# One layer of a hybrid encoder on one core: the Hyena branch's last gate and output kept with channels on partitions, its RMS factor applied when the output projection leaves PSUM

## The chip, the core and the metric

The kernel runs on one core of a Trainium2 chip. The core has a matrix engine (TensorE, PE in the profile; its weight loads are a row of their own, PEld), a vector engine (VectorE, DVE), a scalar engine (ScalarE, ACT), GpSimd (POOL), which here only issues DMAs that add into their destination or load weights, and SyncE (SP), which issues most of the other DMAs. All five run their own list of instructions in order and wait for each other by semaphores. Matmuls write into PSUM; everything else lives in SBUF, on 128 partitions, or in DRAM.

The metric is the device time of one execution in microseconds (us), as the median of several.

## The reference, cut to what matters

Sequence length 1024, model width 1024, batch 1, all in float32. Both branches are 512 channels wide; each is RMS-normalised over its 512 channels, multiplied by a SiLU gate, and the two together go through one output projection that is added to the input.

```python
h = rms_norm(x, norm_g[l]); proj = h @ w_in[l]
...
u = centred_short_conv(hy_in, conv_w[l], conv_b[l])      # 3 taps
hv, hx1, hx2 = jnp.split(u, 3, axis=-1)
...
z = hx1 * long_conv(hv, k_f[:, 0], hb[0])                # FFT convolution
z = hx2 * long_conv(z, k_f[:, 1], hb[1])
y_h = z
...
y = jnp.concatenate([rms_norm(y_h, hy_out_norm_g[l]) * jax.nn.silu(g_h),
                     rms_norm(y_a, attn_out_norm_g[l]) * jax.nn.silu(g_a)], axis=-1)
x = x + y @ w_out[l]
```

`rms_norm(y_h, g)` is `y_h * rsqrt(mean(y_h**2) + eps) * g`. The factor 1 / rms is one number per token; `g` and the gate act per channel. Since the output projection sums over channels, a factor per token may be applied to the projected row as well.

## The kernel before

**Stages.** `prelude` loads x and makes its high and low float32r parts (a float32 product is made of three float32r matmuls: high times high, high times low, low times high; L257 to L259 for the channel tiles, L508 to L510 for queries, keys and values, L1124 to L1126 for the output projection). Then the input projection runs over 12 Hyena tiles of 128 channels (3 parts n of 4 channel quarters s), 3 query/key/value tiles and 8 gate tiles. At the same time the "branch" runs: for each of four channel quarters the spectrum of the implicit filter, two long convolutions as matmuls with DFT tables (`fw` L761 forward, `inv` L802 inverse, butterflies and products on VectorE), and after the fourth quarter the attention. At the end comes the output projection (`output_part`), 8 token blocks by 2 halves of 512 columns by 2 branches.

**Order.** The program is written as two Python generators, the branch and the projections, that `weave` (L1177) merges: each yields a planned cost, and the branch goes on while `ta * SHARE <= tb + LEAD`. A list scheduler with priorities then places the instructions of each engine in a fixed order. `EARLY` attention units are emitted before the four `hyena_output` calls, and each call yields `HC`. The last three gate tiles are computed together; behind them on POOL's queue stand the loads of the output weights (`woraw`, L1031 and L1049). The attention goes on beside the output projection: each attention unit asks `self.outs` for one more output part. Below, an attention block means the work from one query block's `bT` transposes (L960) to the next one's.

**Tiles of the change.** `short_conv` (L406) makes a Hyena tile with channels on the 128 partitions in `hsc`. Its closure `transposes` (L429), kept in `put_off` and run by `late` one tile later, turns it to tokens on partitions: 8 PE transposes into PSUM (`uT`, L434), two ACT copies (L439) and a store to DRAM (`hy`, L440), from which the branch loads it as `u` (L817). `long_conv` (L750) multiplies the inverse transform by the gate (L803) with tokens on partitions; `hyena_quarter` (L807) squares the result on ACT in 8 instructions with a sum over channels (`zsq`, `zssq`, L834) and stores it (`zd`). `hyena_output` (L1066) loads gate and `zd`, applies SiLU (L1064), multiplies by 1 / rms (L1075), turns the result back by 8 PE transposes (`yT`, L1079), multiplies by channel weight and gate out of PSUM (L1081) and splits into high and low parts `yh` (L1084) and `yl` (L1085). 1 / rms is made at L1288 from `zssq`. `output_part` (L1112) gives the first `FIRST` = 3 token blocks a bank of their own for the Hyena half, which leaves PSUM by itself; for the other five blocks both branches are added up in one bank and leave it once (L1128).

## Time and profile before

| what | value |
|---|---|
| median of 3 runs | 638.59 us (636.98 to 641.66) |
| the profiled execution's own time | 637.56 us |
| its span, from the first to the last instruction | 635.8 us |
| granted TensorE clock | 1.0 all through |
| PE transposes: `uT` / `yT` / `oT` | 96 / 32 / 32 |
| DMA | 98.37 MB, mean 155 GB/s |

A row of a group of instructions reads: line of the kernel, engine, operation, output <- inputs, shapes, count, then busy time in us and the mean duration of one in ns, then the idle time of the engine ahead of them and who ended it. A matmul's duration is longer than the distance to the next one's start, since matmuls overlap in the engine; the chain of waits shows the distances.

### The profile page before, as it was taken

Reading aid. Unit: us, or ns where it says so; the run is one execution under the profiler, and the core shown is the slowest. Engines: PE = TensorE matmul, PEld = TensorE weight load, DVE = VectorE, ACT = ScalarE, POOL = GpSimd, SP = SyncE. Lnnn points to the kernel's source line nnn. Section 1 sums busy time; section 2 is a strip of 40 time slices with the busy share of each in tenths; the row PEclk is TensorE's granted clock in tenths of the full one; section 3 lists DMA queues with packets and bytes.
Section 4 is the critical chain, followed back from the end, with each engine's and each line's share of the span. In section 5 each row is a group of like instructions: output and inputs, shape, how many; then the busy total and the mean of one; then the engine's idle time right before and its main releaser. Section 6 shows DMA issues by size and latency. Waiting matters only on the chain.

```text
span 635.8 us, 10699 instructions
## 1 busy us (share of the span) xinstructions
PE 625.0 (98%) x3994; PEld 553.1 (87%) x3994; DVE 531.2 (84%) x1189; ACT 266.5 (42%) x506; POOL 65.3 (10%) x83
## 2 busy tenths in 40 slices
PE   9999999999999999999999999999998999999997
PEld 7878998989898989899998988888787878888885
DVE  6969699997999997979999899689989888976531
ACT  6766413254432353523443332545465343544210
POOL 0121002021100121211102102100200000000000
PEclk9999999999999999999999999999999999999999
DMA  8966937478574576694548656645645125313321
GB/s 324 281 148 155 296 86 181 126 180 202 147 182 129 148 184 160 138 216 107 134 135 208 184 175 156 188 138 182 207 137 179 56 65 166 105 37 114 100 82 51
DMA packets 47107, 98.37 MB, mean 155 GB/s; under 512 B 6728, under 2 KB 15440, under 8 KB 46800
## 3 DMA queue, kind: packets, MB, share of 16 engines
q1 hardware_dynamic: 32784, 63.79, 30.2%
q0 software_dynamic: 10720, 26.21, 21.8%
q10 hardware_dynamic: 3552, 7.71, 3.5%
q8 instruction: 31, 0.51, 0.3%
q14 instruction: 20, 0.16, 0.1%
HBM read 53.65 MB, written 22.02 MB: 119 GB/s over the span
## 4 chain that ended last, share of the span: by engine, by line
PE 85%; DMA 5%; DVE 4%; issue 3%; ACT 2%; POOL 0%; SPq 0%; POOLq 0%; ACTq 0%; DVEq 0%
PE proj L257 10%; PE proj L258 9%; PE proj L259 9%; PE dft L645 8%; PE pv L1000 5%; PE fw L761 5%; PE po L1124 4%; PE po L1126 4%; PE po L1125 4%; PE inv L802 4%; PE qkv L508 3%; PE qkv L509 3%; PE qkv L510 3%; PE smax L940 1%; PE uT L434 1%
## 5 line engine op out<-in xcount | busy, mean ns | idle before, releaser
L257 PE MATMUL proj<-h,w_hi 128*128 128x512 f32 x304 | 121.5, 400 | 0.0
L259 PE MATMUL proj<-h,w_lo 128*128 128x512 f32 x304 | 119.8, 395 | 0.0
L258 PE MATMUL proj<-h,w_hi 128*128 128x512 f32 x304 | 119.7, 394 | 0.0
L225 POOL DMA_DIRECT2D w_lo<-wraw x48 | 42.2, 896 | 242.3 <-ACT w_lo L224 220.3
L258 PEld LDWEIGHTS proj<-h,w_hi 128*128 128x128 f32 x304 | 57.2, 188 | 11.4 <-issue 0.7
L257 PEld LDWEIGHTS proj<-h,w_hi 128*128 128x128 f32 x304 | 57.2, 188 | 11.3 <-issue 0.7
L259 PEld LDWEIGHTS proj<-h,w_lo 128*128 128x128 f32 x304 | 57.1, 188 | 10.9
L508 PE MATMUL qkv<-w_hi,h 128*128 128x256 f32 x192 | 55.0, 287 | 0.0
L510 PE MATMUL qkv<-w_hi,h 128*128 128x256 f32 x192 | 54.6, 285 | 0.0
L509 PE MATMUL qkv<-w_lo,h 128*128 128x256 f32 x192 | 54.4, 284 | 0.0
L222 ACT CAST w_hi<-wraw 128x512 fp32r<-128x512 f32 x48 | 29.4, 619 | 59.7 <-PE proj L258 36.6
L645 PE MATMUL dft<-eo,d 128*128 128x128 f32 x352 | 45.5, 276 | 1.5 <-DVE eo L629 1.5
L1000 PEld LDWEIGHTS pv<-vv,pf 128*128 128x128 f32 x352 | 44.6, 191 | 2.0 <-DVE ao L1005 0.4
L1000 PE MATMUL pv<-vv,pf 128*128 128x66 f32 x352 | 45.0, 269 | 0.1
L645 PEld LDWEIGHTS dft<-eo,d 128*128 128x128 f32 x352 | 42.5, 192 | 2.0 <-DVE eo L629 1.9
L508 PEld LDWEIGHTS qkv<-w_hi,h 128*128 128x128 f32 x192 | 36.7, 191 | 0.0
L509 PEld LDWEIGHTS qkv<-w_lo,h 128*128 128x128 f32 x192 | 36.7, 191 | 0.0
L510 PEld LDWEIGHTS qkv<-w_hi,h 128*128 128x128 f32 x192 | 36.7, 191 | 0.0
L945 DVE CUSTOM_DVE_ANT_0 mj<-smax,mask 128x384 f32<-128x384 f32 (+1 forms) x64 | 33.2, 519 | 3.7 <-PE smax L940 2.2
L986 ACT ACTIVATE pf<-st 128x768 f32<-128x768 f32 (+1 forms) x32 | 24.3, 758 | 25.5 <-DVE st L983 24.9
L802 PE MATMUL inv<-V,di 128*128 128x128 f32 x256 | 34.8, 275 | 0.0
L1128 DVE TENSOR_TENSOR xr<-po,xr 128x512 f32<-128x512 f32 x22 | 15.1, 688 | 22.0 <-PE po L1126 22.0
(217 smaller groups left out, 1458.2 us busy)
## 6 DMA issues: line engine op xcount, KB each, us to landing
wraw<-in_w_in SPq DMA_DIRECT2D x48, 256.0 KB, 3.7
w_lo<-wraw POOLq DMA_DIRECT2D x48, 256.0 KB, 4.2
hy<-hsc ACTq DMA_DIRECT2D x12, 512.0 KB, 5.9
u<-hy SPq DMA_DIRECT2D x12, 512.0 KB, 6.1
hsc<-hs POOLq DMA_DIRECT2D x9, 511.5 KB, 5.3
hsc<-hraw POOLq DMA_DIRECT2D x9, 511.5 KB, 5.4
x<-in_x_t SPq DMA_DIRECT2D x8, 512.0 KB, 8.9
dec<-in_decay SPq DMA_DIRECT2D x8, 512.0 KB, 4.2
```

The source lines that it names most:

```text
L225: nc.gpsimd.dma_start(l.bitcast(F32), raw, accum_op=ALU.add)
L257: nc.tensor.matmul(pt, hi[:, k], xh, start=k == 0, stop=False)
L258: nc.tensor.matmul(pt, hi[:, k], xl, start=False, stop=False)
L259: i = nc.tensor.matmul(pt, lo[:, k], xh, start=False, stop=k == 7)
L508: nc.tensor.matmul(pt[:, b], hh, hi[:, :, k], start=k == 0, stop=False)
L509: nc.tensor.matmul(pt[:, b], hh, lo[:, :, k], start=False, stop=False)
L510: i = nc.tensor.matmul(pt[:, b], hl, hi[:, :, k], start=False, stop=k == 7)
L645: nc.tensor.matmul(out, m, eo[:, t, e], start=n == 0, stop=n == len(terms) - 1)
L761: nc.tensor.matmul(pt[:, k, c], self.d[:, t + k, c], u[:, t + k], start=True, stop=True)
L802: nc.tensor.matmul(pt[:, k], self.di[:, t + k, c], v[:, t + k, c], start=c == 0, stop=c == 1)
L945: V.tensor_tensor_reduce(out=junk[:, 0:nk], in0=pm[:, 0:nk], in1=mask, op0=ALU.add, op1=ALU.max, scale=1.0, scalar=NEG, accum_out=mx[:, 4 ...
L1000: nc.tensor.matmul(pv[:, h], probs[:, n, cols], self.vv[:, k0 + n, g], start=n == 0, stop=n == nk - 1)
```

## The change

The third part of the Hyena projection (n = 2, the last gate) is no longer transposed. Its put-off closure copies the 1024 tokens into another order on ACT and stores that, one tile later than before, behind the last weight conversion issued. The second long convolution swaps stationary and moving operand of its inverse matmuls, so that its result stands with channels on partitions. The squares become one ACT instruction per quarter, whose result is stored (quarter 0) or added (1 to 3) into one DRAM buffer `zq` by a POOL DMA; `hyena_rms` loads that sum once into the still unused `yl[:, 3]`, adds over channels by 8 matmuls with a column of ones, and makes 1 / rms. `hyena_output` then has an ACT multiply by the channel weight and one VectorE product. Every Hyena half of the output projection leaves PSUM by itself, scaled by 1 / rms per token. `LEAD` goes from 28.531 to 31, `EARLY` from 4 to 3.

```diff
-SHARE, LEAD, FINE, HB = 0.915, 28.531, 2, 100
+SHARE, LEAD, FINE, HB = 0.915, 31, 2, 100
...
-EARLY = 4
+EARLY = 3
...
-                nc.scalar.mul(l, raw, -1.0)
+                self.last_w = nc.scalar.mul(l, raw, -1.0).ins.name
...
-        self.put_off.append((self.tiles + (not own), transposes))
+        def turned():
+            i = nc.scalar.copy(raw.rearrange("p (a b) -> p a b", a=8), taps)
+            self.tc.add_manual_dep(i.ins, self.last_w, self.NOSYNC, reason="behind the weights")
+            nc.scalar.dma_start(self.hy[n, s], raw.rearrange("p (a b) -> p a b", a=8))
+            self.stored += 1
+        self.put_off.append((self.tiles + (not own) + (n == 2), turned if n == 2 else transposes))
...
-                        nc.tensor.matmul(pt[:, k], self.di[:, t + k, c], v[:, t + k, c], start=c == 0, stop=c == 1)
+                        m = self.di[:, t + k, c], v[:, t + k, c]
+                        nc.tensor.matmul(pt[:, k], *(m[::-1] if turned else m), start=c == 0, stop=c == 1)
...
-        for t in range(8):
-            sq = bp.tile([P, 2, CH], F32, tag="gp", name=self.nm("zsq"), bufs=1)[:, 0]
-            nc.scalar.activation(sq, z2[:, t], AF.Square, accum_out=self.zssq[:, s, t : t + 1])
         nc.sync.dma_start(self.zd[s], z2)
+        sq = bp.tile([P, 8, 2, CH], F32, tag="x", name=self.nm("zsq"))[:, 0:4].rearrange("p a c b -> p (a c b)")
+        nc.scalar.activation(sq.rearrange("p (b a) -> p a b", a=8), z2, AF.Square)
+        if s == 0:
+            nc.sync.dma_start(self.zq, sq)
+        else:
+            nc.gpsimd.dma_start(self.zq, sq, accum_op=ALU.add)
...
+    def hyena_rms(self, ap, ps):
+        nc = self.nc
+        zs = self.yl[:, 3].bitcast(F32)
+        nc.sync.dma_start(zs, self.zq)
+        ss = ps.tile([P, 8, 2], F32, tag="t", name=self.nm("zss"))
+        for j in range(8):
+            i = nc.tensor.matmul(ss[:, j, 0:1], zs[:, j * P : (j + 1) * P], self.ones, start=True, stop=True)
+            if j == 0:
+                self.tc.add_manual_dep(i.ins, self.last_st, self.NOSYNC, reason="behind the scores")
+        ztot = ap.tile([P, 8], F32, name="ztot", bufs=1)
+        nc.vector.tensor_copy(ztot, ss[:, :, 0:1].rearrange("p a b -> p (a b)"))
+        self.rh = self.rsqrt(ap, ztot, 8, 1.0 / 512)
...
-        V.tensor_tensor(out=y, in0=y, in1=view(rstd, 0, [[1, 8], [0, P]]), op=ALU.mult)
-        for h in range(2):
-            pt = ps.tile([P, 4, P], F32, tag="t", name=self.nm("yT"))
-            for k in range(4):
-                nc.tensor.transpose(pt[:, k], y[:, 4 * h + k], self.ident)
-            gv = g.rearrange("p (b a) -> p a b", a=8)[:, 4 * h : 4 * h + 4]
-            V.scalar_tensor_tensor(
-                out=gv, in0=pt, scalar=self.gn[:, c : c + 1], in1=gv, op0=ALU.mult, op1=ALU.mult
-            )
+        yt = sp.tile([P, S], F32, tag="raw", name=self.nm("yt"))
+        nc.scalar.mul(yt.rearrange("p (b a) -> p a b", a=8), y, self.gn[:, c : c + 1])
+        V.tensor_tensor(out=g, in0=yt, in1=g, op=ALU.mult)
...
-        if last:
+        if c0 == 0:
+            nc.vector.scalar_tensor_tensor(
+                out=xt[:, cols], in0=po, scalar=self.rh[:, j : j + 1], in1=xt[:, cols], op0=ALU.mult, op1=ALU.add
+            )
+        else:
             nc.vector.tensor_tensor(out=xt[:, cols], in0=po, in1=xt[:, cols], op=ALU.add)
-        if c0 == 4:
             nc.sync.dma_start(self.out[rows, cols], xt[:, cols])
...
                 for c in range(4):
-                    with tc.issue_after(sums.ins):
-                        self.hyena_output(c, rstd, sp, ps_)
+                    with tc.issue_after(self.pin.ins):
+                        self.hyena_output(c, sp)
+                    if c == 2:
+                        self.hyena_rms(ap, ps_)
                     yield HC
```

`self.pin` is the last attention product emitted (L1005) and `self.last_st` the last score matmul emitted (L978); both only set places in the engines' lists.

Three places show how the lists move. The first is PE in the attention after the fourth quarter; `yT` are the transposes of the Hyena output, `zss` the sums over channels, `smax` and `st` scores, `pv` attention values, `proj` the input projection. Before:

```order
L933 MATMUL aT_4166<-identr,qq_3982 128x128 x2
L940 MATMUL smax_4173<-kt_3940,qa_4164 128x384
L1079 MATMUL yT_4352<-consts,y_4349 128x128 x4
L977 MATMUL st_4150<-qa_4018,kt_3940 128x256
L978 MATMUL st_4150<-qb_4069,kt_3941 128x256
```

And after:

```order
L990 MATMUL st_4118<-qb_3967,kt_3830 128x256
L952 MATMUL smax_4077<-kt_3829,qa_4056 128x384
L1086 MATMUL zss_4261<-ones,yl 128x1 x8
L258 MATMUL proj_4303<-h_90,w_lo 128x512
L952 MATMUL smax_4081<-kt_3829,qa_4063 128x384
```

The 32 transposes are gone from this stretch, and at one place in it PE waits for the squares of all four quarters.

The second is POOL at the end of the input projection; `w_lo` is the low part of an input weight, made by an adding DMA, `woraw` an output weight as loaded, `zq` the sum of squares. Before:

```order
L225 DMA w_lo<-wraw_4233 128x512
L1031 DMA woraw_4467<-in_w_out 128x512
L225 DMA w_lo<-wraw_4235 128x512
L1031 DMA woraw_4469<-in_w_out 128x512
L1031 DMA woraw_4502<-in_w_out 128x512
L1049 DMA woraw_4578<-in_w_out 128x1024
```

And after:

```order
L224 DMA w_lo<-wraw_4173 128x512
L1044 DMA woraw_4363<-in_w_out 128x512
L224 DMA w_lo<-wraw_4175 128x512
L1044 DMA woraw_4365<-in_w_out 128x512
L847 DMA zq<-zsq_3788 128x1024
L1062 DMA woraw_4544<-in_w_out 128x1024
L1062 DMA woraw_4538<-in_w_out 128x1024
```

The last quarter's squares stand behind two weight conversions and two output-weight loads, and the other ten output-weight loads stand behind the squares.

The third is VectorE in the attention's second block; `gate` is the Hyena gate tile, `graw` a gate tile leaving PSUM, `wo` an output weight's low part, `y` the Hyena result, `rsy` and `rst` steps of 1 / rms. Before:

```order
L1081 SCALAR_TENSOR_TENSOR gate_4429<-yT_4437,consts,gate_4429 128x4x128
L983 TENSOR_TENSOR st_4552<-st_4552,mask_3929 128x2x256
L1038 TENSOR_TENSOR wo_4466<-woraw_4467,wo_4466 128x512
L1081 SCALAR_TENSOR_TENSOR gate_4429<-yT_4443,consts,gate_4429 128x4x128
L1064 SCALAR_TENSOR_TENSOR gate_4478<-th_4480,gate_4478 128x1024
L1075 TENSOR_TENSOR y_4483<-y_4483,rsy_4331 128x1024
L1085 TENSOR_TENSOR yl<-gate_4429,yh 128x1024
L1081 SCALAR_TENSOR_TENSOR gate_4478<-yT_4486,consts,gate_4478 128x4x128
```

And after:

```order
L1077 SCALAR_TENSOR_TENSOR gate_4248<-th_4250,gate_4248 128x1024
L108 TENSOR_TENSOR rst_4274<-rsy_4275 128x8
L996 TENSOR_TENSOR st_4435<-st_4435,mask_3818 128x2x256
L269 TENSOR_TENSOR graw_4340<-proj_4303,row 128x512
L1104 TENSOR_TENSOR gate_4248<-yt_4255,gate_4248 128x1024
L109 TENSOR_TENSOR rst_4274<-rst_4274,rsh_4273 128x8
L1016 TENSOR_TENSOR den_4421<-pv_4414,es_4128 128x2
L111 SCALAR_TENSOR_TENSOR rsy_4275<-rst_4274,rsy_4275 128x8
```

The products out of PSUM became fewer and plain, but the four Hyena outputs now all stand in this part of the list, together with the steps of 1 / rms; the low parts of the output weights stand later.

## Prediction
> **What bounds the kernel now.** I read the page's busy row first, then the waits of PE, then the chain of waits, then the busy time by stage.

> ```profile
> span 635.8 us, 10699 instructions
> PE 625.0 (98%) x3994; PEld 553.1 (87%) x3994; DVE 531.2 (84%) x1189; ACT 266.5 (42%) x506; POOL 65.3 (10%) x83
> PE 85%; DMA 5%; DVE 4%; issue 3%; ACT 2%; POOL 0%; SPq 0%; POOLq 0%; ACTq 0%; DVEq 0%
> ```

> PE is busy 625.0 of 635.8 us and carries 85% of the chain; VectorE (DVE) has 84%. ACT and POOL are far from full, so an instruction moved to them costs nothing by its length, only by its place in a chain. The waits of PE by what it waited for (us in total, times, longest) are short:

> ```profile
> PE dft L645 <- DVE eo L629: 1.5, 1, 1.5
> PE smax L940 <- DVE mx L945: 1.2, 2, 0.6
> PE st L977 <- ACT pf L986: 1.0, 2, 0.7
> ```

> Together 3.7 us. So the first reading is: PE work taken out comes off the time. The table by stage (start:end, length, then busy us of PE, PEld, DVE, ACT, POOL) qualifies that. Its borders are the `bT` transposes that open a block of the attention:

> ```profile
> 60.00:416.44 356.44, 354.77 (x2418) 324.84 (x2416) 321.57 (x601) 136.87 (x275) 50.04 (x58) 1.00 0.65 167
> 433.00:464.88 31.88, 31.38 (x192) 26.44 (x191) 29.55 (x67) 16.15 (x28) 4.85 (x9) 1.00 0.58 190
> 464.88:493.27 28.39, 25.98 (x164) 21.90 (x163) 25.26 (x81) 16.46 (x30) 0.54 (x1) 1.00 0.50 159
> 493.27:519.34 26.07, 25.54 (x161) 21.43 (x160) 21.09 (x75) 10.36 (x21) 0.00 (x0) 1.00 0.17 51
> 580.04:635.80 55.76, 51.80 (x272) 43.38 (x271) 20.90 (x66) 10.85 (x21) 0.00 (x0) 1.00 0.22 76
> ```

> Before 416 us, in the block from 493 and in the last 56 us PE is full or waits for nothing but the end, and DVE has 10% or more free. In the two blocks from 433.00 to 493.27, where the Hyena outputs are made, both are nearly full: in 60.27 us PE has 57.36 and DVE 54.81. There a gain on PE alone can run into DVE.

> **The change part by part: PE.** The price of a transpose is its distance to the next start. The chain (start, us, what) has whole runs:

> ```profile
> 30.53 1.68 PE xss L179 x16
> 60.87 0.88 PE uT L434 x8
> 422.43 0.44 PE yT L1079 x4
> ```

> Both kinds cost 0.11 us each (0.88 / 8, 0.44 / 4). The change drops 32 `uT` (4 tiles of 8) and all 32 `yT`: 64 x 0.11 = 7.0 us. It adds 8 sums over channels, `zss`, of the same shape as the 8 sums `xss` at the start, which stand as 16 records in 1.68 us: +1.7. Net on PE: -5.3 us. The swapped inverse matmuls stay 128x128 by 128x128, and stationary tiles of either kind are already used (`u`, `V` beside tables), so I cost them at nothing.

> The duration that the trace gives for one (min/median/max in ns, first and last start) is longer:

> ```profile
> L434 PE MATMUL uT<-consts,hsc x96: 272/274/349, 50.9 to 344.7; 128*128 128x128 f32 x96
> ```

> At 274 ns each the 64 would be worth 17.5 us instead of 7.0; since in a run they start 0.11 us apart I keep 7.0, and the other reading is a rival below. [...]

> **VectorE.** The rows of the Hyena output and of the output's evacuation:

> ```profile
> L1081 DVE SCALAR_TENSOR_TENSOR gate<-yT,consts,gate 128x512 f32<-128x512 f32 x8 | 9.9, 1238 | 0.0
> L1075 DVE TENSOR_TENSOR y<-y,rsy 128x1024 f32<-128x1024 f32 x4 | 4.9, 1228 | 0.0
> L1085 DVE TENSOR_TENSOR yl<-gate,yh 128x1024 fp32r<-128x1024 f32 x4 | 4.9, 1221 | 0.0
> L1128 DVE TENSOR_TENSOR xr<-po,xr 128x512 f32<-128x512 f32 x22 | 15.1, 688 | 22.0 <-PE po L1126 22.0
> L111 DVE SCALAR_TENSOR_TENSOR rsy<-rst,rsy 128x8 f32<-128x8 f32 x9 | 1.5, 164 | 0.2
> ```

> Out go 8 strided products out of PSUM (9.9) and 4 multiplies by 1 / rms (4.9). In come 4 plain 128x1024 products at about 1.22 (4.9) and 10 more evacuations, two for each of the five token blocks that used one bank for both branches, at about 0.69 (6.9; that they scale as well costs nothing in the rows of this shape that I have). Net -3.0 us, but unevenly: the 6.9 come after 490 us, where DVE has room.

> The distance of a 512-column matmul to the next start, from the chain in two stretches:

> ```profile
> 53.18 0.23 PE proj L259
> 623.02 0.23 PE po L1124
> ```

> In the two full blocks the list of DVE after the change differs so: 5 of the products out of PSUM and 2 multiplies go (5 x 1.24 + 2 x 1.23 = 8.7), and 4 plain products, one more SiLU (1.22), ten short steps of 1 / rms (10 x 0.16), one gate and one attention evacuation more (2 x 0.69) come: 4.9 + 1.2 + 1.6 + 1.4 = 9.1. The Hyena outputs now stand in a row, so what DVE saves falls into the block before. So DVE needs 54.8 + 0.4 = 55.2 us there, as before, while PE loses there 20 `yT` (2.2), 15 projection matmuls (3.4, moved earlier) and 5 output matmuls (1.1, moved later): 6.7 of its 57.4 (some attention products and transposes besides are about even).
> So the two blocks become DVE's. Their floor is 55.2, that is -5.1; with DVE as full as now (54.81 of 60.27) they would take 60.7, that is +0.4. I take the floor, since PE will stand ready for it and the neighbouring blocks have free DVE time. Outside these blocks PE keeps -5.3 + 6.7 = +1.4 us, all at PE's pace. Sum: -5.1 + 1.4 = -3.7 us.

> **ACT, POOL and the new waits.** ACT rows that change:

> ```profile
> L439 ACT COPY hsc<-uT 128x512 f32<-128x512 f32 x24 | 12.8, 586 | 1.0 <-PE uT L434 0.9
> L834 ACT ACTIVATE zsq<-u 128x128 f32<-128x128 f32 x32 | 9.9, 310 | 12.9 <-DVE u L803 12.3
> L834 ACT ACTIVATION_READ_ACCUMULATOR zsq<-u 128x1 f32 x32 | 6.1, 189 | 0.0
> L169 ACT ACTIVATE x<-x 128x1024 f32<-128x1024 f32 x8 | 8.1, 1044 | 0.0
> ```

> ACT loses 8 copies (4.7) and 32 squares with their reads (16.0); it gains 4 reordering copies, 4 squares and 4 multiplies of 1024, each 1.04 if the strided side costs nothing, 1.9 if it costs what it does on DVE (1238 against 688). That is 12.5 to 22.6 us against 20.7, on an engine that is 42% busy: nothing. The third gate reaches DRAM one tile later; it is read only in the quarter's second convolution, some tens of us on, so I cost that at nothing too.

> Two waits are new. First, the squares borrow the `x` buffer, so the next quarter's butterfly must wait until the adding DMA has read them. The rows before, for one quarter, and the landing time of an adding DMA of this size from the page's list of issues:

> ```profile
> 245.36 0.59 ACT L769 COPY c<-fw 128x512 f32<-128x512 f32 x1 [2.54 <-PE fw L761]
> 252.22 0.42 DVE L734 TENSOR_TENSOR X<-ef 128x256 f32<-128x256 f32 x1
> hsc<-hraw POOLq DMA_DIRECT2D x9, 511.5 KB, 5.4
> ```

> In the second quarter ACT's list has the square behind this copy and one weight cast: 245.95 + 0.62 + 1.04 + 0.86 to issue + 5.4 = 253.9 against 252.2. That is up to 1.7 us of DVE, once, or 2.6 with a slow square; DVE has 10% free in that stage, so 0 to 2.6, and I take 0.

> Second, PE stops at `zss` until the sum has come. On POOL the squares stand behind a run of four like the following, which took 11.7 us from first to last issue (the last row is a load of the sum's size on SP):

> ```profile
> 407.66 0.86 POOL L225 DMA_DIRECT2D w_lo<-wraw  x1 [12.12 <-ACT zsq L834]
> 411.27 0.57 POOL L1031 DMA_DIRECT2D woraw<-in_w_out  x1 [2.74 <-DMA w_lo<-wraw]
> 412.15 0.86 POOL L225 DMA_DIRECT2D w_lo<-wraw  x1 [0.32 <-PE smax L940]
> 419.36 0.57 POOL L1031 DMA_DIRECT2D woraw<-in_w_out  x1 [6.35 <-DMA w_lo<-wraw]
> gate<-gt SPq DMA_DIRECT2D x4, 512.0 KB, 3.5
> ```

> 11.7 + 0.57 + 0.86 + 5.4, then the load of the sum at 0.3 + 3.5: 22.3 us after the first of the four. PE meanwhile runs, by the order after, 68 projection matmuls (68 x 0.23 = 15.6) and some 11 us of inverse, score and attention matmuls, 26 to 27 us, of which ACT's cast and multiply take 1.3 first. So the sum is there 3 to 4 us early: 0, with up to 6 us if both landings are slow. What stands behind PE there is the whole attention; what stands behind `zq` on POOL are the other ten output-weight loads.

> `LEAD` and `EARLY` add no instruction; they set the places counted above.

> **Sum.** -3.7 us on the profiled execution: 637.56 becomes 633.9. That execution lies 1.0 under the median of 638.59, so the median becomes 634.9; I say 635.0. On its own this case runs from 633.3 (PE's whole -5.3) to 640.4 (blocks at +0.4, outside +1.4): 0.42. One per cent, 6.4 us, is about what a measurement of this kernel can tell from no change.

> **Rivals.** *DVE does not bind* (0.30). PE gets the whole -5.3, and the shorter DVE list before and after the two blocks also ends the 3.7 us of waits listed above: -9.0, 629.6. For it: the lighter outputs free 9.9 us of DVE in the stretch where PE waits for `mx` and `pf`. Against it: the count of the two blocks.

> *The time only moves* (0.13). The blocks stay at 60.3 and the PE work that left them is run elsewhere: +1.4, 640.0.

> *The sum comes late* (0.12), the case on the other side. The landings (min/median/max) of `hsc` and of `hy` with its reader:

> ```profile
> DMA to landing us min/median/max: 4.5/5.4/9.8
> DMA to landing us min/median/max: 4.9/5.9/7.9
> ```

> If the adding DMA and the load take the longest of these, 9.8 and 7.9, the sum comes at 31.1 us instead of 22.3, and PE stands 5 to 6 us; the ten output-weight loads behind it move as well, and the output projection, whose first matmuls wait for them, loses about the same again: -3.7 + 11.4 = +7.7, 646.3. It decides from about 10 us of delay in all.

> *A transpose is worth its duration* (0.03). Each of the 64 takes its 274 ns out of PE's time: -17.5 + 1.7 = -15.8, 622.8. Against it stand the runs at 0.11. [...]

> **Chances and range.** Faster by over 1% (under 632.2): 0.27 of the second case, 0.03 of the last and 0.04 from the edge of the first, 0.34. Slower by over 1% (over 645.0): 0.10 of the late sum and 0.02 of unforeseen waits, 0.12. Within: 0.54. The range 628.5 to 642.0 holds the first three cases and leaves out the late sum and the last rival.

> **What would show it.** Right: 64 `uT` and no `yT`, PE busy near 620 us; the two blocks with the Hyena outputs at 55 to 58 us with DVE above 95%; no wait of PE at `zss`; a short wait of DVE's `X` for a DMA. Wrong: a PE wait for `yl<-zq` of some us, PE waits for output weights, or two blocks well under 55 us, which would mean that my count of DVE there is off.

## The result, and the profile after

The changed kernel took 661.52 us (median of 4 runs, 661.38 to 662.28) against 638.23 us for the kernel before: a ratio of 1.0359, 95% interval 1.0317 to 1.040. It is slower by 3.6%, where 635.0 us and most likely no measurable change were predicted. The profiled execution has a span of 659.6 us against 635.8.

The page of the changed kernel, first busy times, then the granted clock of PE in 40 slices, then the shares of the chain:

```profile
span 659.6 us, 10553 instructions
PE 631.7 (96%) x3946; PEld 558.7 (85%) x3946; DVE 530.4 (80%) x1191; ACT 276.7 (42%) x446; POOL 68.0 (10%) x86
PEclk9999999998999999989989999997997899999999
PE 72%; DMA 9%; issue 7%; DVE 7%; ACT 3%; SPq 0%; POOL 0%; ACTq 0%; POOLq 0%; DVEq 0%
```

PE has 48 matmul records less and is yet busy 6.7 us longer, because its clock was not granted in full in six slices (before, every slice had a 9): a 512-column `proj` matmul takes 0.39 us at 276 us, with the clock at 1.00, and 0.63 at 283 us, with 0.50. The chain has moved off PE: 72% where it was 85%, and DMA, DVE and the share without a releaser have grown. PE's waits (us in total, times, longest):

```profile
PE dft L651 <- ACT fc L676: 5.9, 2, 3.2
PE inv L810 <- DVE V L740: 3.3, 1, 3.3
PE po L1145 <- DVE xr L1149: 3.1, 1, 3.1
PE st L989 <- ACT pf L999: 2.4, 1, 2.4
PE po L1145 <- ACT wo L1050: 2.1, 2, 1.4
PE pv L1013 <- DVE mx L963: 1.5, 1, 1.5
```

The longest wait of the kernel before was 1.5 us. Now there are two of 3.2 and 2.6 us for a copy on ACT, one of 3.3 for DVE, one of 3.1 for an eviction, and a cluster near 450 us. The stages, with borders at the `bT` transposes that open a block of the attention, as in the prediction (start:end, length, busy us of PE, PEld, DVE, ACT, POOL, then the granted clock):

```profile
60.00:435.30 375.30, 364.45 (x2418) 331.20 (x2416) 320.50 (x586) 141.93 (x212) 53.22 (x62) 0.99 0.66 169
435.30:451.80 16.50, 14.80 (x111) 13.36 (x111) 9.82 (x39) 7.74 (x19) 0.00 (x0) 1.00 0.10 33
451.80:518.50 66.70, 57.26 (x311) 48.81 (x312) 55.61 (x159) 37.57 (x60) 5.41 (x10) 0.85 0.48 162
518.50:606.90 88.40, 87.50 (x578) 76.10 (x577) 72.72 (x261) 39.16 (x77) 0.00 (x0) 1.00 0.28 91
606.90:659.60 52.70, 48.96 (x254) 40.85 (x252) 24.15 (x67) 9.93 (x18) 0.00 (x0) 1.00 0.24 81
```

Before the first block +18.9 us (375.30 against 356.44), in the two blocks with the Hyena outputs +6.4 (66.70 against 60.27), and the three others together -1.5. Most of the loss lies in the stage of which the prediction spoke least.

As a sum over PE: its last matmul ends at 655.9 us against 632.0, 23.9 later. The gaps between its matmuls from 30 us on add up to 22.9 against 5.6, +17.3. The time at the lowered clock, read from the windows in steps of 1 us and weighted with PE's busy share, is 13.7 us against none. That leaves -7.1 us for the work itself; -5.3 was predicted. So the saving is there, and waits and a lowered clock bury it.

What the waits come from is read from the lists of the waiting engines. ACT near 155 us (start, us, what, idle time ahead and its releaser):

```profile
150.59 0.33 ACTq L439 DMA_DIRECT2D hy<-hsc  x1
151.02 1.15 ACT L421 ACTIVATE hs<-hraw,consts 128x1024 f32<-128x1024 f32 x1 [0.46 <-DVE hraw L269]
156.18 1.24 ACT L411 ACTIVATE hsc<-hraw,consts 128x1024 f32<-128x1024 f32 x1 [4.02 <-DMA hy<-hsc]
157.33 0.56 ACT L676 COPY fc<-dft 128x512 f32<-128x512 f32 x1
```

The middle tap of a short convolution waits 4.02 us for a DMA to free its `sc` buffer, and the spectrum copy `fc`, for which PE waits, stands behind it. In the kernel before, the short squares of the quarter and both `fc` stood ahead of that tap, which waited for its buffer too, but with no `fc` behind it:

```profile
156.34 0.59 ACT L670 COPY fc<-dft 128x512 f32<-128x512 f32 x1
166.21 1.25 ACT L412 ACTIVATE hsc<-hraw,consts 128x1024 f32<-128x1024 f32 x1 [2.66 <-DMA hy<-hsc]
```

Near 333 us it is a turned copy, 2.05 us long, ahead of `fc`. The wait of 3.3 us has its origin 16 us earlier, on DVE and POOL:

```profile
253.64 0.87 POOL L847 DMA_DIRECT2D zq<-zsq  x1 [11.04 <-ACT zsq L843]
261.58 0.43 DVE L740 TENSOR_TENSOR X<-ef 128x256 f32<-128x256 f32 x1 [4.15 <-DMA zq<-zsq]
280.58 0.79 PE L810 MATMUL inv<-V,di 128*128 128x128 f32 x4 [3.28 <-DVE V L740]
```

The butterfly's first result `X` waits 4.15 us for the adding DMA that still reads the `x` buffer, and what DVE loses there PE loses at the next inverse.

### The profile page after: what moved, and what is told of

It reads as the page before. It is cut to its first block, busy times and chain, and to the rows that moved or that the text cites. A ratio compares the mean times of both kernels' runs of the same rounds, so it can differ in the third digit from the quotient of the medians.

```text
span 659.6 us, 10553 instructions
## 1 busy us (share of the span) xinstructions
PE 631.7 (96%) x3946; PEld 558.7 (85%) x3946; DVE 530.4 (80%) x1191; ACT 276.7 (42%) x446; POOL 68.0 (10%) x86
## 3 DMA queue, kind: packets, MB, share of 16 engines
q0 software_dynamic: 11152, 27.78, 22.3%
## 4 chain that ended last, share of the span: by engine, by line
PE 72%; DMA 9%; issue 7%; DVE 7%; ACT 3%; SPq 0%; POOL 0%; ACTq 0%; POOLq 0%; DVEq 0%
PE proj L256 8%; PE proj L257 8%; PE proj L258 8%; PE dft L651 6%; PE pv L1013 5%; PE po L1145 4%; PE po L1146 4%; PE po L1147 4%; PE fw L768 3%; PE qkv L515 2%; PE qkv L514 2%; PE qkv L516 2%; PE inv L810 2%; DMA wraw<-in_w_in 2%; PE st L990 2%
## 5 line engine op out<-in xcount | busy, mean ns | idle before, releaser
L256 PEld LDWEIGHTS proj<-h,w_hi 128*128 128x128 f32 x304 | 58.0, 191 | 12.5 <-DVE hraw L269 1.0
L516 PE MATMUL qkv<-w_hi,h 128*128 128x256 f32 x192 | 54.8, 285 | 0.0
L514 PE MATMUL qkv<-w_hi,h 128*128 128x256 f32 x192 | 54.8, 285 | 0.0
L651 PE MATMUL dft<-eo,d 128*128 128x128 f32 x352 | 47.6, 285 | 5.9 <-ACT fc L676 5.9
L651 PEld LDWEIGHTS dft<-eo,d 128*128 128x128 f32 x352 | 44.4, 199 | 7.2 <-ACT fc L676 6.5
L1013 PEld LDWEIGHTS pv<-vv,pf 128*128 128x128 f32 x352 | 46.3, 196 | 3.3 <-issue 2.3
L223 ACT ACTIVATE w_lo<-wraw 128x512 fp32r<-128x512 f32 x48 | 29.9, 627 | 11.2 <-PE qkv L515 11.2
L1145 PE MATMUL po<-wo,yh 128*128 128x512 f32 x64 | 27.0, 422 | 5.2 <-DVE xr L1149 3.1
## 6 DMA issues: line engine op xcount, KB each, us to landing
u<-hy SPq DMA_DIRECT2D x12, 512.0 KB, 5.6
hsc<-hs POOLq DMA_DIRECT2D x9, 511.5 KB, 6.9
hsc<-hraw POOLq DMA_DIRECT2D x9, 511.5 KB, 5.5
x<-in_x_t SPq DMA_DIRECT2D x8, 512.0 KB, 7.8
dec<-in_decay SPq DMA_DIRECT2D x8, 512.0 KB, 5.2
hy<-hsc ACTq DMA_DIRECT2D x8, 512.0 KB, 4.6
```

The lines of the kernel that those rows point to most:

```text
L223: self.last_w = nc.scalar.mul(l, raw, -1.0).ins.name
L256: nc.tensor.matmul(pt, hi[:, k], xh, start=k == 0, stop=False)
L514: nc.tensor.matmul(pt[:, b], hh, hi[:, :, k], start=k == 0, stop=False)
L516: i = nc.tensor.matmul(pt[:, b], hl, hi[:, :, k], start=False, stop=k == 7)
L651: nc.tensor.matmul(out, m, eo[:, t, e], start=n == 0, stop=n == len(terms) - 1)
L1013: nc.tensor.matmul(pv[:, h], probs[:, n, cols], self.vv[:, k0 + n, g], start=n == 0, stop=n == nk - 1)
```

## The experiments

Theory A: single instructions that wait for a DMA, ahead of what PE needs on an in-order list, cost the time. Its rivals are P (the planner's two numbers) and B (DVE has more to do, so that a wait removed comes back elsewhere). Theory C, beside A, says that PE's waits also lower the clock behind them; against it stand D (that chip or run) and E (the attention's small matmuls). Ratios are to the kernel before, with 95% intervals; the changed kernel has 1.0359, and differences from it are worked out from the two ratios.

**LEAD and EARLY as before.**

```diff
-SHARE, LEAD, FINE, HB = 0.915, 31, 2, 100
+SHARE, LEAD, FINE, HB = 0.915, 28.531, 2, 100
-EARLY = 3
+EARLY = 4
```

> The changed kernel with LEAD 28.531 and EARLY 4 as before; nothing else. Theory A (single instructions that stand on an in-order list ahead of what PE needs, and wait there for a DMA, cost the time): all of them are still in the lists, so 655 to 662 us and about as many PE waits of over 2 us as the changed kernel's. Rival P (the planner's two numbers put the work too far ahead): 636 to 642 us, at most two PE waits of over 2 us left.

660.86 us, 1.0321 (1.0248 to 1.0394). The waits at 154 and 278 us stay (3.4 and 3.3); the one at 333 is gone, and 3.0 at 464, 3.4 at 493 and 2.3 at 504 us are new. The two numbers move waits about; putting them back doesn't take the loss away.

**No adding DMA.** The sum over channels then leaves out the squares of three quarters.

```diff
-        if s == 0:
+        if s == 3:
             nc.sync.dma_start(self.zq, sq)
-        else:
-            nc.gpsimd.dma_start(self.zq, sq, accum_op=ALU.add)
```

> The changed kernel without the three adding DMAs of the squares: quarters 0 to 2 leave their squares out of DRAM, the last quarter stores its own, so the sum is that of one quarter. Theory A: the 3.3 us wait of PE near 277 us, which came from the wait of X for the buffer that the adding DMA held, is gone, with the slow stretch behind it: 5 to 7 us less than the changed kernel, about 655 us. Rival B (the waits are slack that something else fills, the time comes from DVE having more to do): the stall moves elsewhere, 659 to 662 us.

655.64 us, 1.0265 (1.0192 to 1.0339): about 6 us less, but its four executions lie between 652 and 661 us and the two intervals overlap. What is clear is the trace: the wait at 277 us and its slow stretch are gone, the others stay. Theory A holds for this wait; that B falls for it rests on the run with the adds from DRAM to DRAM below.

**The third gate stored without the extra tile of delay.**

```diff
-        self.put_off.append((self.tiles + (not own) + (n == 2), turned if n == 2 else transposes))
+        self.put_off.append((self.tiles + (not own), turned if n == 2 else transposes))
```

> The changed kernel with the third gate turned and stored as early as before (without the extra tile of delay). Theory A: the short convolution near 151 us then finds its sc buffer free earlier, and the copy that PE waits for (3.2 us at 155) isn't held up: the first long wait of PE is gone, 4 to 6 us less, 655 to 657 us; the turned copy, about 2 us, still stands in ACT's list ahead of the spectrum's copies near 333 us. Rival: the wait there belongs to the short convolution's own DMAs and stays, 660 to 663 us.

660.38 us, 1.0339 (1.0288 to 1.0391). The wait near 155 us stays (3.7): the delay of the gate isn't its cause. The waits at 277 and 333 us go, and one of 6.1 us for `fc` comes at 246. ACT there:

```profile
248.72 2.02 ACT L444 COPY hraw<-hsc 128x1024 f32<-128x1024 f32 x1 [13.41 <-DMA hsc<-hraw]
250.77 0.33 ACTq L446 DMA_DIRECT2D hy<-hraw  x1
251.14 0.58 ACT L676 COPY fc<-dft 128x512 f32<-128x512 f32 x1 [0.40 <-ACT hraw L444]
```

My reading was wrong in the instruction, not in the kind: here a turned copy that waits for the convolution's adding DMA, with `fc` behind it.

**Two stalls put into the kernel before**, in its last 25 us, where nothing else disturbs.

```diff
+        hold = {(6, 1, 4): 13, (7, 1, 0): 3}.get((j, n, c0))
...
+            nc.scalar.copy(ht, pd[:, 0])
+            for _ in range(hold):
+                nc.scalar.copy(ht, ht)
```

> The kernel before with two waits of PE put into its last 25 us: a matmul waits for a chain of ACT copies, once long (14 copies of 128 columns, about 4 us), once short (4 copies, about 1.2 us). The output is the same. Theory C (a long wait of PE also lowers the granted clock for some us after it): after the long one the output matmuls start 0.43 us apart instead of 0.23 for 3 to 7 us, after the short one they stay at 0.23; in all 4 + 1.2 + 2 to 3 us more than before, 643 to 645 us. Rival D (the lower clock in the changed kernel is a matter of that chip or run, not of the waits): 0.23 throughout, 641 to 642 us.

650.39 us in its one execution, 12 more than before. PE after the long stall and after the short one:

```profile
625.88 0.79 PE L1128 MATMUL hold<-consts,ht 128*128 128x128 f32 x2 [4.64 <-ACT ht L1126]
626.90 0.63 PE L1138 MATMUL po<-wo,ah 128*128 128x512 f32 x1
627.33 0.63 PE L1139 MATMUL po<-wo,al 128*128 128x512 f32 x1
...
630.74 0.62 PE L1138 MATMUL po<-wo,ah 128*128 128x512 f32 x1
631.17 0.43 PE L1139 MATMUL po<-wo,al 128*128 128x512 f32 x1
...
635.96 0.49 PE L1128 MATMUL hold<-consts,ht 128*128 128x128 f32 x2 [1.34 <-ACT ht L1126]
636.52 0.39 PE L1138 MATMUL po<-wo,yh 128*128 128x512 f32 x1
636.75 0.39 PE L1139 MATMUL po<-wo,yl 128*128 128x512 f32 x1
```

The rows with an idle time in brackets are the matmuls that wait for a chain of copies; the `po` rows behind them are output matmuls. Behind 4.64 us of waiting the output matmuls start 0.43 us apart for 4.8 us, then 0.23 again; behind 1.34 us they keep 0.23. Theory C holds among these 512-column matmuls: the long wait costs itself and a slow stretch (here 2.7 us by the clock), the short one costs itself alone. The total is some 5 us above the expectation: 0.9 more of waiting ahead of the chain, waits of 1.7 and 1.0 us near 458 and 471, where the kernel before has one of 0.7, and the added matmuls.

**Two places of ACT's list**: one middle tap and one turned copy go behind the two spectrum copies of their time.

```diff
+        if (n, s) == (0, 2):
+            self.behind_fc(i, 0, 1)
...
+            if s == 3:
+                self.behind_fc(i, 0, 3)
...
```

> The changed kernel with two places of ACT's list altered and nothing else: the middle tap of the short convolution of tile (0, 2) and the turned copy of tile (2, 3) now stand behind the two spectrum copies that PE's transforms wait for, instead of ahead of them. Theory A (single instructions that wait for a DMA, ahead of PE's need on an in-order list): the PE waits of 3.2 us near 155 us and 2.6 us near 333 us are gone, with the slow stretch behind each, 7 to 9 us less than the changed kernel, 652 to 655 us. Rival B (DVE has more to do and is the cause; a wait that is removed comes back elsewhere): 658 to 662 us.

653.64 us, 1.0238 (1.0208 to 1.0267): 7.7 us less, within the 7 to 9 expected. Near 155 us no wait is left, near 327 one of 0.8. The edit asks for two places in one list and nothing else, but the scheduler, which places by priorities, then moved 93 of PE's 3946 matmuls and 16 instructions on DVE's list as well; so the 7.7 us are the price of the two places with what followed from them.

**The squares added from DRAM to DRAM.**

```diff
-        if s == 0:
-            nc.sync.dma_start(self.zq, sq)
-        else:
-            nc.gpsimd.dma_start(self.zq, sq, accum_op=ALU.add)
+        nc.sync.dma_start(self.zq[s], sq)
+        if s:
+            nc.gpsimd.dma_start(self.zq[0], self.zq[s], accum_op=ALU.add, max_dma_last_dim=1024)
...
```

> The changed kernel with each quarter's squares stored plainly by SP, in a DRAM tile of their own, and added there from DRAM to DRAM by POOL's queue, so that the x buffer is read by a plain store alone. Theory A: the store lands some 4 us after the squares instead of 7.9, the 3.3 us wait of PE near 277 us goes, 4 to 7 us less than the changed kernel, 655 to 658 us, as without the adding DMA. Rival B: 659 to 662 us. A third way: the adds from DRAM to DRAM are slow, the last of them ends late and the sum over channels has to be waited for by PE near 445 us: 660 us or more, with a wait at zss.

653.31 us, 1.0241 (1.0201 to 1.0281): 7.5 us less, a little under the 655 to 658 expected. DVE's list is the same as in the changed kernel, so B falls for this wait. The wait at 277 us is gone, and there is none at `zss`, so the sum still comes in time.

**The rows of x one block ahead.**

```diff
-                    xt[j] = self.output_x(j, xp)
+                    for i in (j, j + 1) if j >= FIRST - 1 else (j,):
+                        if i < 8 and i not in xt:
+                            xt[i] = self.output_x(i, xp)
```

> The changed kernel with the rows of x for a token block loaded one block ahead, so that the load stands ahead of the next block's gates on SP's queue. Theory A: the 3.1 us wait of PE near 512 us (output matmul, for the eviction that waited for the rows) is gone with its slow stretch: 4 to 5 us less than the changed kernel, 656 to 658 us. Rival B: 660 to 662 us.

661.20 us, 1.0352 (1.0318 to 1.0386): nothing, and the wait is still there (2.9). The loads are first in the program's text but not on SP's queue. The changed kernel's queue:

```profile
501.05 0.32 SPq L909 DMA_DIRECT2D qkv<-qd  x1
503.54 1.21 SPq L884 DMA_DIRECT2D tab<-in_rope  x2
505.74 0.38 SPq L1119 DMA_DIRECT2D ga<-gt  x1
506.22 0.45 SPq L1122 DMA_DIRECT2D of<-od  x1
506.72 0.43 SPq L1119 DMA_DIRECT2D ga<-gt  x1
507.19 2.19 SPq L1110 DMA_DIRECT2D xr<-in_x  x4
```

All four loads stand behind a `qkv` load that itself waits 11.9 us for DVE's `kk`; in the kernel before they left at 473 to 475 us, ahead of `qkv`. I had moved the wrong thing.

**All three edits, and the multiplies by the gain of the second to fourth output held back on ACT.**

```diff
+        if c:
+            for name in self.last_pf, self.last_qb:
+                self.tc.add_manual_dep(i.ins, name, self.NOSYNC, reason="behind the probabilities")
```

> All three edits together, and the multiplies by the gain of the second to fourth Hyena output behind the probabilities and the second transposes' copies on ACT's list. Theory A: the single waits add up, each with its slow stretch: 7 to 9, 5 to 7, 4 to 5, and 4 to 6 for the waits of 1.5, 0.7 and 2.4 us near 450: 20 to 27 us less than the changed kernel, 635 to 642 us, with the mean granted clock back at 0.99 or more. Rival B (DVE bounds the stage, and waits taken away come back elsewhere): over 648 us.

646.89 us, 1.0143 (1.0103 to 1.0183), above the 635 to 642 expected. PE's gaps fall to 9.8 us, yet the mean clock is 0.975, not 0.99. The windows of 4 us (PE busy is the second number, the clock the third from the end):

```profile
416.00:420.00 4.00, 2.39 (x17) 1.49 (x15) 2.39 (x13) 0.75 (x3) 0.00 (x0) 1.00 0.82 124
420.00:424.00 4.00, 3.13 (x18) 2.90 (x19) 1.65 (x4) 3.00 (x10) 0.00 (x0) 0.58 0.64 213
424.00:428.00 4.00, 4.00 (x22) 4.00 (x22) 1.51 (x6) 2.11 (x5) 0.00 (x0) 0.50 0.05 18
432.00:436.00 4.00, 4.00 (x19) 4.00 (x20) 1.21 (x5) 0.00 (x0) 0.00 (x0) 0.50 0.00 0
444.00:448.00 4.00, 3.58 (x12) 3.10 (x13) 3.66 (x9) 3.89 (x7) 0.00 (x0) 0.50 0.67 179
448.00:452.00 4.00, 4.00 (x27) 3.56 (x27) 2.77 (x6) 3.43 (x4) 0.00 (x0) 1.00 0.94 312
```

Waits of 1.3 and 0.4 us between 417 and 420, neither of them long, are followed by 27 us at half clock from 420.7 on, 12 us lost; a third wait, of 0.8 us, falls into it. No projection matmul starts between 417.0 and 444.4 us, where they fill PE in the changed kernel; that the hold kept their stage buffers occupied is my reading of the program, not shown.

**The same with a hold for the third and fourth output alone, one attention unit later**; then a second profile of it.

```diff
-        if c:
+        if c > 1:
...
+                    if c == 1:
+                        yield next(attn)
```

> The kernel with all edits again, but only the third and fourth multiply by the gain are held behind the probabilities on ACT's list, after one attention unit; the second stays early, so that the stage buffers it reads come free and the projections that fill PE at the first bT transposes stay there. Theory A with C (each wait, or cluster of waits, costs itself and whole slow windows of 3.4 us behind it; the eight slow windows of the run before, from 420 to 448 us, came from the cluster of 2.5 us in waits at 417 to 422, where those projections were missing): no slow window before 480 us, 12 us less than with all edits before, 633 to 639 us. Rival E (the stage itself, with small matmuls, holds the clock down whatever stands ahead of it): slow windows stay there, 643 to 648 us.

650.87 us, 1.0168 (1.0148 to 1.0187), a miss.

> The kernel that took 650.9 us instead of the 633 to 639 expected; its profiled execution was one at 874 us with the clock at 0.65 throughout and shows nothing of the others. Theory C: a profile at about 650 us shows four or more slow windows of 3.4 us, each stretch behind a cluster of PE waits of 2 us or more within some 5 us, at a place where the list changed. Rival F: the clock is at 0.99 or more and the time is in waits of PE, 12 us more of them than in the kernel before.

649.36 us in one execution, clock 0.978: eight slow windows (stretches of 3.41 us at half clock), 11.4 us lost in all, as theory C expected. They stand near waits of 1.97 us at 429, of 1.0 and 1.9 at 448 to 458, and of 0.6 and 1.1 at 495 us, but not all behind them: the second stretch begins at 447.8 us, ahead of the wait of 1.0 at 448.1; the gaps are 6.3 us over those of the kernel before. The projections are back at 420 us, but now the scores wait for probabilities.

**The three edits (ACT's two places, adds from DRAM to DRAM, rows of x) without any hold, with LEAD and EARLY as before**, and then **with those of the change**:

> The changed kernel with the two ACT places, the adds from DRAM to DRAM and the rows of x as in the runs above, without any hold of the gain multiplies, and with LEAD 28.531 and EARLY 4 as before. Theory A: the two waits before 300 us are gone; in the attention the waits that stood in the run with LEAD and EARLY alone (3.0 us near 464, 3.4 and 1.1 near 495, 2.3 near 504) stay, 644 to 650 us. Rival P (with the old numbers the stage needs no hold): 636 to 641 us.

> The changed kernel with the two ACT places, the adds from DRAM to DRAM and the rows of x one block ahead, without any hold of the gain multiplies. Theory A: the waits near 155, 277 and 333 us are gone with their slow windows, 8 + 7 us less than the changed kernel, 645 to 648 us; those of 1.5, 0.7 and 2.4 us near 445 and their three slow windows stay. Rival B: over 652 us.

658.48 us, 1.0301 (1.0278 to 1.0324), and 647.25 us, 1.0100 (1.0069 to 1.0131). The second is as theory A says: no wait of 1 us before 433 us, the cluster from 433 to 441 stays with three slow windows. The first misses upward by 8 us: new waits of 2.5, 2.1 and 3.6 us, and 19.4 us of slow clock in all, half of it behind waits of no more than 0.7 us. The two differ in LEAD and EARLY alone, so here the numbers of the change are the better ones, by 11 us of the medians.

The second also shows PE's saving alone. The rows of the inverse matmuls name the starts of the first and of the last one; before, in the changed kernel, and here:

```profile
L802 PE MATMUL inv<-V,di x256: 270/275/377, 102.5 to 402.5; 128*128 128x128 f32 x128
L810 PE MATMUL inv<-di,V x128: 270/275/421, 144.6 to 420.3; 128*128 128x128 f32 x128
L818 PE MATMUL inv<-di,V x128: 270/275/377, 143.7 to 405.2; 128*128 128x128 f32 x128
```

Ahead of the last one stand 794, 827 and 825 projection matmuls. For the repaired kernel 405.2 - 402.5 - 31 x 0.23 = -4.4 us, of which 0.5 are shorter waits; 32 transposes fewer at 0.11 were to give -3.5. The changed kernel is 15 us later than the repaired one with 2 matmuls more: that is the price of the three waits, 8.5 us of waiting and 5.1 of slow clock.

**The planner's numbers alone, in the kernel before.**

```diff
-SHARE, LEAD, FINE, HB = 0.915, 28.531, 2, 100
+SHARE, LEAD, FINE, HB = 0.915, 31, 2, 100
-EARLY = 4
+EARLY = 3
```

> The kernel before with LEAD 31 and EARLY 3, its only edit: the planner's part of the change alone. Theory A: the lists shift by a few places and nothing that waits for a DMA is added, so 637 to 642 us and no PE wait over 2 us. Rival P: over 645 us, with waits of PE as in the changed kernel.

644.97 us, 1.0086 (1.0062 to 1.0109). Between both theories: two numbers that add no instruction cost 5.5 us. The gaps grow by 1.6 us only; three slow windows behind waits of 2.1 and 1.3 us cost 5.1. A single wait of 1.3 us, which cost nothing more among the output matmuls, has two of them behind it here in the attention.

**Unused matmuls in the waits** of the 646.89 us kernel.

```diff
+        held = self.fill(12, last, ps) if j == 0 else None
...
+        held = self.fill(8, self.last_st, ps) if (j, g, hp) == (0, 0, 1) else None
```

> The kernel of the run with all edits (646.9 us), with 20 matmuls of 128x128 added that compute nothing used: 12 ahead of the first bT transposes, 8 ahead of the second score matmuls, the places at 417 to 422 us where PE waited 1.3, 0.4 and 0.8 us. The waits stay, PE is only busy in them. Theory C (PE's idle share in a window of 3.4 us sets the clock of the next ones): the eight slow windows from 420 to 448 us are gone, 10 to 13 us less, 634 to 638 us, which is under the kernel before. Rival E (the small matmuls of the attention hold the clock down, whatever stands ahead): 646 to 650 us, slow windows at the same place.

644.44 us, 1.0086 (1.0054 to 1.0117). The same windows as above:

```profile
416.00:420.00 4.00, 4.00 (x27) 3.15 (x26) 3.12 (x15) 0.15 (x1) 0.35 (x1) 1.00 0.76 117
420.00:424.00 4.00, 3.56 (x36) 3.40 (x35) 1.02 (x2) 2.49 (x6) 0.00 (x0) 1.00 0.52 145
424.00:428.00 4.00, 3.89 (x38) 3.73 (x37) 1.67 (x6) 1.52 (x5) 0.00 (x0) 1.00 0.33 104
432.00:436.00 4.00, 3.49 (x19) 2.77 (x19) 3.29 (x14) 0.00 (x0) 0.00 (x0) 0.74 0.00 0
```

With PE kept busy the clock stays at 1.00 from 420 to 432, over the same attention matmuls that ran at half before, so these do not hold it down whatever stands ahead, as rival E has it. But E is not out: four slow windows begin at 433.9 us, ahead of a wait of 2.55 us at 437, behind sums over channels (`zss`, one column each) and attention matmuls in which PE had not waited over 0.2 us since 428.7. It was not the whole 10 to 13 us, since the 20 matmuls took 4.3 us where PE had waited 2.5, and since these four windows stay.

**Fewer there, and eleven ahead of the second `bT`.**

```diff
-        held = self.fill(12, last, ps) if j == 0 else None
+        held = self.fill((7, 11)[j], last, ps) if j < 2 else None
...
-        held = self.fill(8, self.last_st, ps) if (j, g, hp) == (0, 0, 1) else None
+        held = self.fill(4, self.last_st, ps) if (j, g, hp) == (0, 0, 1) else None
```

> The kernel of the filled run (644.4 us) with fewer unused matmuls at the first two places (7 and 4 in place of 12 and 8, since 12 took 2.6 us where the wait had been 1.7 in all, and 8 took 1.7 where it had been 0.8) and 11 new ones ahead of the second block's bT transposes, where PE waited 2.55 us at 437 us and four slow windows followed. Theory C: no slow window before 480 us, 5.3 us less for the clock and some 1.8 us less for the filling, 636 to 639 us: as the kernel before (639.5) or a little faster. Against it: slow windows stay between 433 and 448 us, 642 to 646 us.

643.52 us, 1.0072 (1.0048 to 1.0096): the clock is at 0.993 and the expected 636 to 639 are missed. Two slow windows stay, from 437.7 to 444.6 us. They begin ahead of the wait of 1.1 us, which starts at 437.9; in the 3.4 us before them, with the 16 `zss` matmuls, PE was busy throughout:

```profile
436.00:437.00 1.00, 1.00 (x11) 1.00 (x11) 0.17 (x1) 1.00 (x2) 0.00 (x0) 1.00 0.00 0
437.00:438.00 1.00, 0.91 (x9) 0.74 (x8) 0.32 (x1) 1.00 (x1) 0.00 (x0) 0.87 0.00 0
```

So theory C, by waits alone, does not account for these windows. PE's last matmul ends 4.8 us after that of the kernel before: 4.7 us of filling + 2.6 more of gaps + 2.9 of slow clock - 5.4. The remainder of 5.4 is near the saving that the prediction put at 5.3; that DVE's chain behind `mx` keeps it from showing there is argued, not shown. No version that I ran beats the kernel before.

## Why the prediction was wrong, point by point

- *PE, -5.3 us.* Right in size: -4.4 measured of -3.5 ahead of the attention (0.5 of it shorter waits), and remainders of -7.1 (changed kernel) and -5.4 (filled one) for the whole.
- *"ACT ... costs nothing by its length, only by its place in a chain."* The step that failed first. I wrote the condition and then summed lengths only. The places cost 7.7 us: the 32 short squares of the kernel before were gone, and the middle tap and a turned copy moved ahead of `fc` on ACT's list. Asking for both behind it returned the 7.7.
- *The wait for the `x` buffer, "0 to 2.6, and I take 0".* Right mechanism, wrong size and wrong cover. DVE waited 4.15 us: the square took 2.1 us, the DMA 7.8 to land instead of 5.4. "DVE has 10% free in that stage" is an average; it had none of it between that wait and PE's next inverse. Price: about 7.5 us.
- *No term for the granted clock.* The profile of before shows it at 1.00 throughout, and I took it as constant. In the changed kernel 13.7 us go there, more than half of the loss.
- *The two blocks, -5.1 as DVE's floor.* They took 66.7 us. DVE was busy 55.6, as counted (55.2), but stood behind waits; the gain multiply on ACT, 2.2 us long, stands ahead of the probabilities for which the scores wait. The floor was no forecast.
- *The sum at `zss`, 0; the rival of the late sum.* No wait at `zss`. The output weights do come late (first load of the second half at 469 us against 447), but by the trace POOL's first one waits 42 us for a gate's store to free a stage buffer, and two of the next for the outputs' `yl`; none waits for `zq`. PE does wait 2.6 us for the weights `wo`, a sign that the prediction named, but from this other cause.
- *"LEAD and EARLY add no instruction; they set the places counted above."* True, and worth +5.5 us in the kernel before and some -11 in the repaired one: places, too, have a price, and not a fixed one.
- *The evictions of the Hyena half*, costed by length (6.9 us of DVE with room): their new need is the rows of x, whose loads came some 33 us later on SP. That makes the wait of 3.1 us; I had not named that queue. Why the loads fall behind `qkv` I didn't isolate.

So I forecast work by its durations on an engine that was full to 98%, and left out that the waits which the change brings are paid nearly twice, with 13.7 us of lowered clock on top of 17.3 us of waiting. What the attention still loses in the repaired kernels, some 5 us in the best of them, stays open in part.

## What to carry to other kernels

On a kernel whose PE is full, list for each engine what stands ahead of the instruction that PE waits for next, and for each such instruction the DMA that it waits for; durations saved on an idle engine can change that list and cost more than they save, as the two places on ACT's list did here with 7.7 us. Look at the granted clock beside every wait, and price a long wait, or a cluster of shorter ones, with the slow windows behind it: in the changed kernel four waits of 2.6 to 3.3 us had one slow window each behind them, and two waits of 1.4 and 0.5 us near 498 us had two. Then check that the slow window begins behind the wait, since some here began ahead of it (in the kernel with 20 unused matmuls at 433.9 us, ahead of the wait of 2.55 at 437). An average of free time is no cover: a cover is named with the instruction that would be late next.

## What the runs showed of the hardware

```text
1.71 (3.2 us wait, changed kernel, 155)      3.42 (4.64 us wait, stall put in, 621)
5.12 (cluster from 449, changed kernel)      13.65 (1.3 and 0.4 us, all edits, 418)
```

They are 1, 2, 3 and 8 times 1.71 us, half of 3.41. In the 3.41 us ahead of each of the six stretches of the changed kernel PE was busy for 0.59 to 1.72 us. With all edits two waits of 1.3 and 0.4 us were followed by the 27 us at half clock, and the clock stayed there through 424 to 428 and 432 to 436 us, in which the records have PE busy for all of the 4.00 us. Behind the 4.64 us put into the output matmuls it came back after two windows of 3.41 us. Why it stayed at half over the small attention matmuls, no run tests. A count over windows of 3.41 us in sixteen of the traces, from 60 us on, points at columns: of 108 slow windows, 56 are followed by another, and in 18 of these PE was busy for 95% or more. Counting the columns that the matmuls starting in a window stream (512 for an output matmul, 66 for a `pv`, 1 for a `zss`) parts them better: 44 of the 56 have under 2400, but only 3 of the 52 behind which the full clock came back. Likewise 49 of the 52 windows at full clock that a slow one follows have under 2350, and 10 of the 2564 others; in the changed kernel these windows ahead of its six stretches have 384 to 2114. That is a correlation; no run varied the columns alone.

An ACT instruction with one strided side of 128x1024 (turned copy, square, multiply by the gain) took 2.05 to 2.33 us in the changed kernel, where contiguous ones of the size take 1.04 to 1.25: a little over the upper of the two prices that the prediction gave.
